# The last store of a row-wise squared deviation, split in two halves on two queues

## The chip, the cores and the metric

One core of a Trainium2 chip. The metric is the device time of one execution in microseconds, the lower the better. Kernels that are compared ran on the same chip, in alternation.

## The reference

```python
def reference(x, axis):          # x: 1024 x 4096 float32, axis = -1
    mean = np.mean(x, axis=axis, keepdims=True)
    return ((x - mean) ** 2).astype(np.float32)
```

16.78 MB are read and 16.78 MB written. There is little arithmetic for each byte.

## The kernel before

Two tiles of 128 partitions; each partition holds four rows of 4,096 numbers (65,536 B). Both tiles are loaded at the start and stay in memory. For each row VectorE sums it into a negative mean and ScalarE squares in place; of each tile's fourth row VectorE squares the last 512 columns. Each tile is stored with one DMA. Cut to what the argument touches:

```python
    for i in range(ntiles):                       # ntiles = 2
        x_tile = io.tile([P, Q * D], F32)         # Q = 4 rows, D = 4096
        if i == 0:
            nc.sync.dma_start(out=x_tile[:, :HEAD], in_=x_t[i][:, :HEAD])
            nc.sync.dma_start(out=x_tile[:, HEAD:], in_=x_t[i][:, HEAD:])
        else:
            end = Q * D - HEAD
            nc.scalar.dma_start(out=x_tile[:, end:], in_=x_t[i][:, end:])
            nc.sync.dma_start(out=x_tile[:, :end], in_=x_t[i][:, :end])
    ...
    for i in range(ntiles):
        for q in range(Q):
            row = tiles[i][:, q * D:(q + 1) * D]
            ...                                   # VectorE: neg_mean of the row
            cut = D if q < Q - 1 else LAST
            nc.scalar.activation(out=row[:, :cut], in_=row[:, :cut],
                                 func=ACT.Square, bias=neg_mean, scale=1.0)
            ...                                   # VectorE: the rest of row 3
        nc.sync.dma_start(out=out_t[i], in_=tiles[i])
```

Of the kernel before, what the change touches and what calls it, by code (L numbers as in the profile page):

```python
# [2 lines left out]

os.environ.setdefault("NEURON_RT_ULTRASERVER_MODE", "4")

# [4 lines left out]

F32 = mybir.dt.float32
ACT = mybir.ActivationFunctionType
ADD = mybir.AluOpType.add


@with_exitstack
def kernel(
    ctx: ExitStack,
    tc: tile.TileContext,
    x: bass.AP,  # L20
    axis: bass.AP,
    out: bass.AP,
):





    nc = tc.nc

    B, D = x.shape
    P = nc.NUM_PARTITIONS
    Q = 4
    HEAD = 512
    HALF = D // 2
    LAST = D - D // 8
    assert B % (P * Q) == 0
    ntiles = B // (P * Q)
    inv_d = 1.0 / float(D)

    x_t = x.rearrange("(p n q) d -> n p (q d)", p=P, q=Q)
    out_t = out.rearrange("(p n q) d -> n p (q d)", p=P, q=Q)

    io = ctx.enter_context(tc.tile_pool(name="io", bufs=ntiles))
    scratch = ctx.enter_context(tc.tile_pool(name="scratch", bufs=1))
    stats = ctx.enter_context(tc.tile_pool(name="stats", bufs=ntiles * Q))

    tiles = []
    for i in range(ntiles):
        x_tile = io.tile([P, Q * D], F32)  # L50
# [7 lines that stand above are left out]
        tiles.append(x_tile)  # L58

    inorder = tc.keep_in_program_order  # L60
# [3 lines that stand above are left out]
            pairs = scratch.tile([P, HALF], F32)  # L64
            neg_mean = stats.tile([P, 1], F32)
            inorder(nc.vector.tensor_tensor_reduce(  # L66
                out=pairs,
                in0=row[:, :HALF],
                in1=row[:, HALF:],
                scale=-inv_d,  # L70
                scalar=0.0,
                op0=ADD,
                op1=ADD,
                accum_out=neg_mean,
            ))
            cut = D if q < Q - 1 else LAST
            nc.scalar.activation(  # L77
                out=row[:, :cut],
                in_=row[:, :cut],
                func=ACT.Square,  # L80
                bias=neg_mean,
                scale=1.0,
            )
            if cut < D:
                rest = row[:, cut:]
                nc.vector.tensor_scalar_add(out=rest, in0=rest, scalar1=neg_mean)  # L86
                nc.vector.tensor_mul(out=rest, in0=rest, in1=rest)  # L87
        nc.sync.dma_start(out=out_t[i], in_=tiles[i])


# [1 line left out]
_INS = ['x', 'axis']  # L92
_OUTS = [((1024, 4096), 'float32')]

_NUMBERS = {'axis': -1}


# [26 lines left out]
```

## Time and profile before

| | before |
|---|---|
| time | 82.98 us (82.96 to 83.04, 3 runs) |
| span of the profile | 81.4 us |
| ScalarE busy, VectorE busy | 36%, 26% |
| share of 16 DMA engines' time, both queues | 96.1% |
| first store: issued, landed | 39.7, 61.2 us |
| second store: issued, landed | 58.4, 80.6 us |

"Issued" is when the issuing engine's instruction starts; "landed" is when the completion arrives. A packet is one record of a DMA engine's work in the profile; in the large stores it is one unbroken piece of a partition's data (65,536 B in the kernel before). A completion is how a DMA reports its end: 16 records of 4 B in the profile (96 of them for the six DMAs of the kernel before), and one wait in the program. The seam is the place where the packets of the first store end and those of the second begin. The time between holds all waiting behind other transfers, so a long one is no sign of a slow transfer (the second store took 22.2 us here). The lines of the page, the windows across the seam of the stores and the waits of SyncE stand in the prediction below.

### The profile page before, as it was taken

How to read it: one execution, taken by the hardware profiler on the slowest of the kernel's cores; microseconds unless marked ns; L12 is line 12 of the kernel's file. 1: busy time of each engine (PE TensorE's matmuls, PEld its weight loads, DVE VectorE, ACT ScalarE, POOL GpSimd, SP SyncE). 2: the span in 40 equal slices, each digit the busy share in tenths (PEclk: the TensorE clock that was granted, in tenths of full speed). 3: DMA queues.
4: the chain of work that ended last, by engine and by line, in shares of the span. 5: the costliest groups of instructions: out<-in, count | busy, mean ns of one | idle time of the engine just before them, and what ended most of it. 6: DMA issues, size and time to landing. Idle time of an engine off the chain costs nothing.

```text
span 81.4 us, 87 instructions
## 1 busy us (share of the span) xinstructions
DVE 20.8 (26%) x20; ACT 29.4 (36%) x9; POOL 0.2 (0%) x4
## 2 busy tenths in 40 slices
DVE  0000000000059999600039999700000000000000
ACT  0000000000054999999502999999600000000000
POOL 0000000000000000000000000000000000000000
DMA  1974999999759999995799993899996599999390
GB/s 22 704 343 187 499 499 499 499 499 437 343 218 499 499 499 499 499 406 250 343 516 515 515 515 161 354 515 515 515 516 290 258 483 515 515 515 419 161 451 0
DMA packets 864, 33.55 MB, mean 412 GB/s; under 512 B 96, under 2 KB 96, under 8 KB 352
## 3 DMA queue, kind: packets, MB, share of 16 engines
q1 hardware_dynamic: 720, 33.29, 95.0%
q10 hardware_dynamic: 144, 0.26, 1.1%
HBM read 16.78 MB, written 16.78 MB: 412 GB/s over the span
## 4 chain that ended last, share of the span: by engine, by line
DMA 49%; ACT 13%; ACTq 4%; DVE 3%; SPq 1%; issue 0%
DMA x_tile<-in_x_dram 49%; ACT x_tile L77 13%; ACTq L119 4%; DVE pairs L66 3%; SPq L53 1%; SPq L52 0%; DVE neg_mean L66 0%
## 5 line engine op out<-in xcount | busy, mean ns | idle before, releaser
L77 ACT ACTIVATE x_tile<-x_tile,neg_mean 128x4096 f32<-128x4096 f32 (+1 forms) x8 | 28.2, 3590 | 5.7 <-DVE neg_mean L66 5.7
L66 DVE CUSTOM_DVE_ANT_0 pairs<-x_tile 128x2048 f32<-128x2048 f32 x8 | 18.3, 2292 | 31.6 <-DMA x_tile<-in_x_dram 31.4
L77 ACT ACT_TABLE_LOAD x1 | 1.3, 1283 | 23.2 <-DMA x_tile<-in_x_dram 23.2
L87 DVE TENSOR_TENSOR x_tile<-x_tile 128x512 f32<-128x512 f32 x2 | 1.4, 692 | 0.1
L86 DVE TENSOR_SCALAR x_tile<-x_tile,neg_mean 128x512 f32<-128x512 f32 x2 | 1.0, 488 | 0.1
L66 DVE DVE_READ_ACCUMULATOR2_ANT neg_mean<- 128x1 f32 x8 | 0.7, 82 | 0.0
L105 POOL MEMSET const-bfloat16-1.0<- 128x1 bf16 x1 | 0.1, 102 | 0.0
L105 POOL MEMSET const-uint8-127<- 128x1 uint8 x1 | 0.1, 102 | 0.0
L105 POOL MEMSET const-float32-0.0<- 128x1 f32 x1 | 0.1, 99 | 0.2 <-issue 0.2
L105 POOL MEMSET const-float32-1.0<- 128x1 f32 x1 | 0.1, 99 | 0.0
## 6 DMA issues: line engine op xcount, KB each, us to landing
x_tile<-in_x_dram SPq DMA_DIRECT2D x2, 7936.0 KB, 31.1
x_tile<-in_x_dram ACTq DMA_DIRECT2D x1, 256.0 KB, 3.8
x_tile<-in_x_dram SPq DMA_DIRECT2D x1, 256.0 KB, 3.6
out_dram<-x_tile SPq DMA_DIRECT2D x2, 21.9
```

The costliest lines, as they stand in the source:

```text
L53: nc.sync.dma_start(out=x_tile[:, HEAD:], in_=x_t[i][:, HEAD:])
L66: inorder(nc.vector.tensor_tensor_reduce(out=pairs, in0=row[:, :HALF], in1=row[:, HALF:], scale=-inv_d, scalar=0.0, op0=ADD, op1=ADD, accu ...
L77: nc.scalar.activation(out=row[:, :cut], in_=row[:, :cut], func=ACT.Square, bias=neg_mean, scale=1.0,)
L86: nc.vector.tensor_scalar_add(out=rest, in0=rest, scalar1=neg_mean)
L87: nc.vector.tensor_mul(out=rest, in0=rest, in1=rest)
L105: nc = _bacc.Bacc("TRN2", target_bir_lowering=False, num_devices=1)
L119: with _tile.TileContext(nc) as tc:
```

## The change

The second tile's store waits for all four rows. Its first two rows are final 6.8 us earlier. The change stores them as soon as they are ready, from SyncE's queue, and the other two from ScalarE's, whose engine has nothing more to do then. The intent is an earlier start of the last store and two issuers.

```diff
-        nc.sync.dma_start(out=out_t[i], in_=tiles[i])
+        if i < ntiles - 1:
+            nc.sync.dma_start(out=out_t[i], in_=tiles[i])
+        else:
+            for queue, q in ((nc.sync, 0), (nc.scalar, 2)):
+                part = slice(q * D, (q + 2) * D)
+                queue.dma_start(out=out_t[i][:, part], in_=tiles[i][:, part])
```

## The prediction

> **What bounds the kernel now.** I read the page first: the busy shares, the slices of the DMA engines, the queues.
>
> ```profile
> DVE 20.8 (26%) x20; ACT 29.4 (36%) x9; POOL 0.2 (0%) x4
> ...
> DMA  1974999999759999995799993899996599999390
> ...
> DMA packets 864, 33.55 MB, mean 412 GB/s; under 512 B 96, under 2 KB 96, under 8 KB 352
> ...
> q1 hardware_dynamic: 720, 33.29, 95.0%
> q10 hardware_dynamic: 144, 0.26, 1.1%
> ```
>
> No compute engine is busy for more than 36% of the span. The two queues' packets fill 95.0 + 1.1 = 96.1% of the time of all 16 DMA engines. The bytes are fixed: 16.78 MB in, 16.78 MB out. So the kernel is bound by its transfers, and the question is whether any of the missing 4% lies where the second tile's store begins.
>
> The slice row seems to say so: it dips to 5 and 3 in several places, one of them at slices 29 and 30 (59 to 63 us), where the first store ends and the second begins. I did not trust this. Of the 864 packets 352 are small, so the other 512 carry nearly everything: 65,536 B each, one for each of 128 rows of four large transfers, 8 per engine per transfer. A packet takes over 2 us, longer than a slice of 2.03 us, so a packet counted in the slice where it starts makes false peaks and dips. I therefore asked for windows as long as one packet, 2.41 us, across the seam (columns: window, length, DVE, ACT, POOL, clock, DMA share, GB/s).
>
> ```profile
> 52.49:54.90 2.41, 0.00 (x0) 2.41 (x1) 0.00 (x0) 1.00 1.00 435
> 54.90:57.31 2.41, 0.00 (x0) 2.41 (x2) 0.00 (x0) 1.00 1.01 435
> 57.31:59.73 2.42, 0.00 (x0) 1.02 (x1) 0.00 (x0) 1.00 1.00 433
> 59.73:62.14 2.41, 0.00 (x0) 0.00 (x0) 0.00 (x0) 1.00 1.01 435
> 62.14:64.56 2.42, 0.00 (x0) 0.00 (x0) 0.00 (x0) 1.00 1.00 433
> ```
>
> The DMA share is 1.00 and the rate 433 to 435 GB/s in every window, before, at and after the seam. There is no hole. The instructions on the output and SyncE's waits say the same in another way:
>
> ```profile
> L88 SPq DMA_DIRECT2D out_dram<-x_tile x2: 343/346/348, 39.7 to 58.4; - x2
> ...
> DMA to landing us min/median/max: 21.5/21.9/22.2
> ```
>
> ```profile
> SPq L119 <- DMA out_dram<-x_tile: 21.7, 2, 19.3
> ```
>
> The stores were issued at 39.73 and 58.36 us (timeline). SyncE's waits at the end are 21.7 us in two parts, 2.4 and 19.3. So the first store landed some 2.4 us after the issue of the second was over (58.7 + 2.4 = 61.1 to 61.2, which is 39.7 + 21.5), and the second 19.3 us later, at 80.6 (58.4 + 22.2). One store is 128 x 65,536 B = 8.39 MB; at 434 GB/s that moves in 19.3 us. From one landing to the next there passed just the time that the bytes need. The second store took 22.2 us because for its first 2 to 3 us it stood behind the first.
>
> [...] The trace of before has a small case: in the first 3.5 us a 256 KB load from SyncE and one from ScalarE run together, and land in 3.6 and 3.8 us.
> [...] The trace doesn't show the order, but in the window 3.10 to 3.30 us, when 2,048 B packets of both queues are in flight, 410 GB/s moved, so changing queues costs at most little.
> [...]
>
> **The change, part by part.**
> - Removed: one store of 8.39 MB, issued by SyncE at 58.36 us when ScalarE ended row 3 of the second tile.
> - Added first: a store of rows 0 and 1 from SyncE. ScalarE's two activations end 7.31 us after 44.25 (chain of waits), so it can be issued at about 51.6 us, if its wait is for the part and not for the tile. I expect that, since these rows lie in columns that nothing later writes; no view of before shows it, and a rival below takes the other case. It is issued 6.8 us earlier, but the first store's packets fill all engines until about 60.9 us (landing at 61.2). It stands in the same queue behind them: gain 0.
> - Added second: a store of rows 2 and 3 from ScalarE, at 58.36 us, after its own last activation. The first load was issued at 0.73 and the first bytes flowed in the window 1.50 to 2.00, so an issue takes about 1.0 us to become traffic: the packets are there at about 59.4, before the engines are free. This was so for the old store too. Gain 0, loss 0. ScalarE has no work after it, so the 0.34 us of issue costs nothing.
> - Moved: nothing else; loads, compute and the first store stay.
> - Packet sizes: each of the 128 rows is now two packets of 32,768 B, so 8 packets more per engine. What a packet costs beyond its bytes, as an estimate: 2,048 B x 16 at 410 GB/s is 79.9 ns, at 434 GB/s 75.5 ns, so 4.4 ns. 8 x 4.4 = 0.035 us.
> - End: one more completion to wait for at the end, but both halves end together; SyncE's waits there take 17 to 28 ns each. About 0.03 us, an estimate.
> - Sum: 82.98 + 0 + 0.035 + 0.03 = 83.05 us.
>
> **The rivals.**
> - *The early half fills a hole at the seam.* The two dips in the slices speak for it, and an issue that waits for the last activation looks like a serial step. It would be worth up to the 1.0 us from issue to first bytes: 82.0 us. Against it: 433 to 435 GB/s in the window across the seam, and 19.3 us between landings for 19.3 us of bytes. Even so it would be under 2%.
> - *Two queues in turn are slower than one.* Engines would jump between two streams of writes 32 KB apart, with packets half as long. The trace has only the small packets of the first 3.5 us to judge by. In the stretch 41.9 to 61.3, where the first store begins among the last packets of a load, the mean is 432 GB/s, so mixing loads and stores cost almost nothing. If each changeover cost 50 ns, 16 of them would make 0.8 us: 83.8 us. To lose over 2% (1.66 us) the last 19.3 us would have to run 8.6% slower. Unlikely.
> - *The second issue waits longer on ScalarE's queue* (behind its last activation, on semaphores of VectorE and itself). It has about 0.9 to 1.5 us of slack before the engines are free, and even past that the early half keeps them busy: half a store is 9.7 us. This makes nothing of the time: 83.0 us.
> - *The early half waits for the whole tile after all.* Then both issues come at 58.4 us, and it is still 83.0 us.
>
> **Range and chances.** The three runs of before span 0.08 us; most of what I can think of moves the time by under 0.1 us. I take 82.85 to 83.40: the upper side is wider because only the changeover rival has size, and it can only lose. Faster by over 2% would need 81.3 us, that is, most of what lies outside the moving of bytes: 33.55 MB at 434 GB/s are 77.3 us of a span of 81.4, and the remaining 4.1 us are the start before the first bytes, the landings and the end, which the change doesn't touch. I give it 0.01. Slower by over 2%: 0.03. Within 2%: 0.96.
>
> **What would show each step.** In the changed profile: queue q1 with 29.1 MB and q10 with 4.46 MB (0.26 + 4.19), 1,008 packets in place of 864; SyncE's issue at about 51.6 us, some 28 us before it lands; ScalarE's at about 58.4 us with about 22 us to landing; both landing within about 1.3 us of each other near 80.6 (queues in turn), where a strict order of first come would land the early half at about 71; windows of 2.41 us at 433 to 435 GB/s throughout; the span at 81.4 to 81.5 us. I am wrong if the windows after 61 us show well under 430 GB/s (changeover cost), or if the last landing comes before 80.5 us (there was a hole after all).

What no trace or run of this case shows is cut from it and from one expectation below. No term of the sum is among the cuts: 82.98 + 0 + 0.035 + 0.03 = 83.05 us. That the queues would go in turn rested on one of the passages cut; the trace of the kernel before did not show the order, and the packet records of the changed kernel do ("Why the prediction was right").

## The result, and the profile after

| | before | changed |
|---|---|---|
| median | 82.98 us (82.93 to 83.04, 6 runs) | 83.15 us (83.05 to 83.33, 6 runs) |
| ratio | | 1.0022, 95% interval 1.0009 to 1.0035 |
| span of the profile | 81.4 us | 81.6 us |

Ratios here and below are the mean time of one kernel's fast runs over that of the other's of the same rounds, so not quite the ratio of the medians that stand beside them. The change costs 0.18 us (0.0022 x 82.98; interval 0.07 to 0.29), which counts as the same time at the 2% mark.

The page of the changed kernel, for packets and queues:

```profile
DMA packets 1008, 33.55 MB, mean 411 GB/s; under 512 B 112, under 2 KB 112, under 8 KB 368
...
q1 hardware_dynamic: 720, 29.10, 83.0%
q10 hardware_dynamic: 288, 4.46, 12.9%
```

The same bytes go in 144 packets more, of which 128 are data (128 rows in two pieces each) and 16 tiny ones are the added completion. ScalarE's queue q10 now has 4.46 MB. The sum of both shares is 95.9%, where it was 96.1%: the engines were full and they still are.

The instructions on the output in the changed kernel, then its list of DMA issues (issuing queue, count, KB, us from issue to landing):

```profile
L90 SPq DMA_DIRECT2D out_dram<-x_tile x1: 348/348/348, 39.6 to 39.6; - x1
L94 SPq DMA_DIRECT2D out_dram<-x_tile x1: 343/343/343, 51.5 to 51.5; - x1
L94 ACTq DMA_DIRECT2D out_dram<-x_tile x1: 347/347/347, 58.2 to 58.2; - x1
```

```profile
out_dram<-x_tile SPq DMA_DIRECT2D x1, 4096.0 KB, 28.0
out_dram<-x_tile ACTq DMA_DIRECT2D x1, 4096.0 KB, 22.4
```

The early half was issued 6.8 us before the late one, as intended. It then took 28.0 us to land, at 79.5 us; the late half took 22.4 us, to 80.7 us. The head start was spent waiting. The windows across the seam in the changed kernel show behind what (columns as in the prediction: window, length, DVE, ACT, POOL, clock, DMA share, GB/s):

```profile
54.90:57.31 2.41, 0.00 (x0) 2.41 (x2) 0.00 (x0) 1.00 1.00 435
57.31:59.73 2.42, 0.00 (x0) 0.91 (x1) 0.00 (x0) 1.00 1.00 433
59.73:62.14 2.41, 0.00 (x0) 0.00 (x0) 0.00 (x0) 1.00 1.01 435
```

The rates are the same three as before. (Of the seven windows that follow, one has 421 GB/s, the others 433 to 435. One packet of 32,768 B that falls across a window's edge is 13.6 GB/s of such a window.) The engines were at 433 to 435 GB/s with the first store's packets when the early half joined the queue, and no byte went sooner.

### The profile page after: what moved, and what is told of

The parts are those of the page before. It is cut to its first block, busy times and chain, and to the rows that moved or that the text cites. A ratio compares the mean times of both kernels' runs of the same rounds, so it can differ in the third digit from the quotient of the medians.

```text
span 81.6 us, 89 instructions
## 1 busy us (share of the span) xinstructions
DVE 20.8 (25%) x20; ACT 29.4 (36%) x9; POOL 0.2 (0%) x4
## 3 DMA queue, kind: packets, MB, share of 16 engines
q10 hardware_dynamic: 288, 4.46, 12.9%
## 4 chain that ended last, share of the span: by engine, by line
DMA 49%; ACT 14%; issue 3%; DVE 3%; SPq 1%
DMA x_tile<-in_x_dram 49%; ACT x_tile L78 14%; DVE pairs L67 3%; SPq L54 1%; SPq L53 0%; DVE neg_mean L67 0%
## 6 DMA issues: line engine op xcount, KB each, us to landing
out_dram<-x_tile ACTq DMA_DIRECT2D x1, 4096.0 KB, 22.4
```

## The experiments

My theory: the second store starts when the engines are free of the first, not when it is issued, so an earlier issue is worth nothing, and what the change adds is the cost of more packets and of one more completion. Rivals: there was a hole at the seam; turning between two queues costs; the last issue sets the end. Twelve runs were made: eleven new kernels, and the changed kernel once more. "Before" is each time the kernel before in the same rounds; its median was 83.12, 83.17 and 83.12 us on the chips of the three sets.

### Is there a hole at the seam, and is the last issue on the path?

**The second store issued 18 us early, with the first tile's data** (wrong result):

```diff
-        nc.sync.dma_start(out=out_t[i], in_=tiles[i])
+        nc.sync.dma_start(out=out_t[i], in_=tiles[0])
```

> Wrong result on purpose: the second store takes the first tile's data, which are ready at 39.7 us, so it is issued some 18 us early and stands complete in the queue before the first store ends; one store, one completion, 64 KB packets. Theory (no hole at the seam before): 82.98 within 0.06 us, ratio 0.999 to 1.001, last landing at 80.5 to 80.7 us. Rival (the late issue of the second store leaves a hole of up to 1 us in the kernel before): 82.0 to 82.7 us.

Measured: 83.11 us, ratio 0.9997 (0.9985 to 1.0009). The store was issued at 40.1 us and landed at 80.5 us, 40.4 us later:

```profile
L88 SPq DMA_DIRECT2D out_dram<-x_tile x2: 347/390/433, 39.7 to 40.1; - x2
...
DMA to landing us min/median/max: 21.5/31.0/40.4
```

Taking the wait for the data away wholly is worth nothing measurable, so the kernel before had no hole to fill. This is the strongest single evidence: the early half of the change couldn't have gained either.

**The last activation delayed by 1 us**, in the kernel before (an added activation of 1,024 columns into a scratch tile, ahead of the second tile's row 3):

```diff
+            if i == ntiles - 1 and q == Q - 1:
+                nc.scalar.activation(out=junk[:, :1024], in_=row[:, :1024],
+                                     func=ACT.Square, bias=neg_mean, scale=1.0)
             cut = D if q < Q - 1 else LAST
```

> The kernel before with an added activation of 1,024 columns ahead of the second tile's last row: the store's issue moves from 58.4 to about 59.4 us. Theory: the store has 0.9 to 1.5 us of slack before the engines are free (60.2 to 60.9), so at most 0.15 us slower: 82.98 to 83.13 us. Rival (the store's issue is on the path that sets the end): +1.0 us, 84.0 us.

Measured: 83.22 us, ratio 1.0003 (0.9985 to 1.0020). The issue moved to 59.6 us and the time did not:

```profile
L97 SPq DMA_DIRECT2D out_dram<-x_tile x2: 343/346/348, 39.8 to 59.6; - x2
```

An issue that can be late by 1.2 us is not on the path.

**The same with 4,096 columns**, in the kernel before and in the changed one:

> The kernel before with an added activation of 4,096 columns (3.6 us): issue at 62.0 us, first packets at about 63.1, while the last engine is free at 60.9. Theory: +2.0 to +2.7 us, 85.0 to 85.7 us, with a window of 2.4 us after 60.9 almost empty. Rival (some other slack hides it): under +1 us.

> The changed kernel with the same added activation of 3.6 us ahead of the last row: ScalarE's issue moves to about 61.9 us, the early half is unmoved at 51.5 us and keeps the engines busy for 9.7 us from 60.2 on. Theory: the delay is hidden wholly: 83.1 to 83.3 us, as the changed kernel without the delay. Rival (the end hangs on the last issue): 85 to 87 us.

Measured: the kernel before went to 85.47 us, ratio 1.0268 (1.0247 to 1.0288), that is 2.23 us longer; the changed kernel to 83.27 us, ratio 1.0010 (0.9993 to 1.0027) to the undelayed kernel before. The windows at the seam, first of the kernel before with the delay, then of the changed kernel with it:

```profile
57.41:59.82 2.41, 0.96 (x2) 2.38 (x2) 0.00 (x0) 1.00 1.00 435
59.82:62.23 2.41, 0.22 (x1) 2.29 (x1) 0.00 (x0) 1.00 0.00 0
62.23:64.64 2.41, 0.00 (x0) 0.00 (x0) 0.00 (x0) 1.00 1.02 435
```

```profile
57.31:59.73 2.42, 0.88 (x2) 2.39 (x2) 0.00 (x0) 1.00 1.00 433
59.73:62.14 2.41, 0.30 (x1) 2.37 (x1) 0.00 (x0) 1.00 0.95 408
62.14:64.56 2.42, 0.00 (x0) 0.00 (x0) 0.00 (x0) 1.00 1.01 433
```

This is what a real hole looks like in this view: a window in which no packet starts, 0 GB/s. In the kernel before the delayed store was issued at 62.1 us while the engines ran dry from 60.4 to 60.9 us. In the changed kernel the early half fills that place. So the split does what it was made for, but only where the last rows come late; here they come in time. The 408 is an edge effect of a few half-size packets that start on either side of the window's edge.

Finer windows of the delayed kernel before time the start of a store's traffic:

```profile
62.70:62.90 0.20, 0.00 (x0) 0.00 (x0) 0.00 (x0) 1.00 0.00 0
62.90:63.00 0.10, 0.00 (x0) 0.00 (x0) 0.00 (x0) 1.00 9.21 3932
```

Issue at 62.14, first packets between 62.9 and 63.0 (62.98 in the packet records): 0.84 us. With the last engine free at 60.9 us, the store of the kernel before, issued at 58.4, had 60.9 - 0.84 - 58.4 = 1.7 us of slack.

### What do the queues cost?

**Both halves on SyncE's queue:**

```diff
-            for queue, q in ((nc.sync, 0), (nc.scalar, 2)):
+            for queue, q in ((nc.sync, 0), (nc.sync, 2)):
```

> Both halves on SyncE's queue, rows 0-1 issued at about 51.5 us, rows 2-3 at about 58.3 us. Theory (the engines have no hole at the seam; the +0.17 us of the change is 8 more packets per engine at some 5 ns and one more completion to wait for at the end): as the changed kernel within 0.1 us, so 83.05 to 83.2 us, ratio to the kernel before 1.0005 to 1.003; the halves come one after the other, the first lands near 71 us, the second near 80.6. Rival (turning between two queues is what costs): back to 82.98 us within 0.04, ratio below 1.0008.

Measured: 83.38 us, ratio 1.0033 (1.0010 to 1.0057), 0.27 us over before with an interval of 0.08 to 0.47. The halves landed at 71.0 and 80.7 us, one after the other. The rival (two queues are the cost) would have brought this back to before; it did not. But the six runs spread from 83.05 to 83.80 us, more than any other kernel here, and the median missed the expected 83.2 us. By the times it says only that two queues are not needed for the cost. The traces say more: the packets of the second store take the engines 19.42 us here, and 19.39 and 19.41 us in the two profiles of the changed kernel (table below), so turning between two queues shows no cost of its own in the changed kernel.

**The early half on ScalarE's queue, right after row 1; the late half on SyncE's:**

```diff
+            if i == ntiles - 1 and q == 1:
+                nc.scalar.dma_start(out=out_t[i][:, :2 * D], in_=tiles[i][:, :2 * D])
 ...
+            nc.sync.dma_start(out=out_t[i][:, 2 * D:], in_=tiles[i][:, 2 * D:])
```

> The early half goes out on ScalarE's queue right after row 1, the late half on SyncE's: the early half then does not stand behind the first store but shares the engines with it in turn from about 52.5 us. Theory (only the sum of bytes counts): the first store lands later, at about 68 to 70 us in place of 61.2, the last at 80.6 to 80.9, and the time is as the changed kernel within 0.15 us, 83.0 to 83.3 us; ScalarE may lose up to 0.5 us at the issue. Rival (mixing queues slows the engines): over 83.5 us.

Measured: 83.20 us, ratio 1.0003 (0.9986 to 1.0021). On a queue of its own the early half did not stand behind the first store; it went in turn with it. Its first packets began 4.2 to 6.6 us after its issue, for each engine first ended the packet it was at and one or two more of the first store. Landing times of the three stores in that kernel:

```profile
DMA to landing us min/median/max: 22.2/25.2/26.4
```

The first store (issued at 39.6) landed at 64.8 us, some 3.5 us later than before, the early half (51.5) at 77.9, the late one (58.3) at 80.5. The time is the same, so the order in which the bytes went didn't matter here, only their sum. My 68 to 70 us for the first store was wrong: I shared the engines out by bytes, and from 52.5 us on. They went in turn by packet. On the three engines that came last the first store still had two 64 KB packets and its completion to send, and in the packet records each of the three stands behind one 32 KB packet of the other queue: 3 x 1.2 = 3.6 us.

### What do packets and completions cost?

**Eight stores of half a row**, four on each queue:

```diff
-            for queue, q in ((nc.sync, 0), (nc.scalar, 2)):
-                part = slice(q * D, (q + 2) * D)
+            for n in range(8):
+                queue = nc.sync if n < 4 else nc.scalar
+                part = slice(n * D // 2, (n + 1) * D // 2)
```

> Eight stores of half a row each, four on SyncE's queue, four on ScalarE's: 16,384 B packets, 32 for each engine where the kernel before has 8, and seven more completions. Theory: 24 x 5 ns = 0.12 us for packets, plus 0 to 0.4 us for the waits at the end (0.06 each if all stand behind the last landing): 83.1 to 83.5 us. Rival (each change of queue costs tens of ns): 32 changes at 50 ns, 1.6 us: above 84 us.

**One store in eight pieces of half a row**, reversed so that the pieces stay apart (64 packets per engine, where the kernel before has 8):

```diff
-            nc.sync.dma_start(out=out_t[i], in_=tiles[i])
+            o = out_t[i].rearrange("p (h d) -> p h d", h=8)
+            s = tiles[i].rearrange("p (h d) -> p h d", h=8)
+            nc.sync.dma_start(out=o[:, ::-1], in_=s[:, ::-1])
 ... (for the second tile; the first tile's store stays)
```

> The second store as one DMA whose rows go out in eight pieces of 8,192 B each, in reversed order, so that they can't be merged: 64 packets per engine in place of 8, the packet size of the eight stores before it, but one completion and one queue. (The 16,384 B and 32 packets named in the expectation of the eight stores were a slip: half a row is 8,192 B.) Theory: 56 packets x 5 to 6 ns = 0.28 to 0.34 us, and no extra wait at the end: +0.25 to +0.4 us, 83.3 to 83.5 us, ratio 1.003 to 1.005. Rival (the queues and completions are the cost of the eight stores, not the packets): within 0.1 us of before. If it is +0.8 us as with the eight stores, packets are the whole of it.

Measured: the eight stores 83.92 us, ratio 1.0097 (1.0083 to 1.0111), 0.81 us over before; the one reversed store 83.73 us, ratio 1.0072 (1.0056 to 1.0088), 0.60 us over before. Both were above what I expected (83.1 to 83.5, and 83.3 to 83.5). In the same 16.90 us after the seam, first of the kernel before, then of the one reversed store, then of the eight stores:

```profile
62.14:79.04 16.90, 0.00 (x0) 0.00 (x0) 0.00 (x0) 1.00 1.00 434
```

```profile
62.14:79.04 16.90, 0.00 (x0) 0.00 (x0) 0.00 (x0) 1.00 1.01 424
```

```profile
62.14:79.04 16.90, 0.00 (x0) 0.00 (x0) 0.00 (x0) 1.00 1.01 421
```

One queue gives 424 GB/s and two queues in turn 421, against 434 with 64 KB packets. So the packets are most of the cost. The changed kernel has 432 GB/s in this window and 434 in its repeat: one of its packets at the edge is 1.9 GB/s, too coarse for so small a cost.

The packet records give a finer measure, with no window's edge in it: the time from the end of the first store's last data packet to the last completion record, as a mean over the 16 engines. Each is one profile; the rows with 8 packets agree within 0.01 us, those with 16 within 0.03.

| kernel | packets per engine | us |
|---|---|---|
| before | 8 | 19.34 |
| halves by even and odd partitions (below) | 8 | 19.33 |
| changed, and its repeat | 16 | 19.39, 19.41 |
| both halves on SyncE's queue | 16 | 19.42 |
| one reversed store | 64 | 19.83 |
| eight stores | 64 | 19.94 |

What one more packet costs comes out as 8 to 11 ns, an estimate in each case. By the times: 0.60 us for 56 more packets per engine is 10.7 ns each (8.3 to 13.1 over the interval). By this table: 0.49 us, 8.8 ns each. By the rates: 8,192 B x 16 x (1/424 - 1/434) = 7.1 ns for each of 64 pieces, so 0.46 us, 8.1 ns for each of the 56 added. Turning between queues at every packet is, by these two profiles, at most the 0.1 us between the last two rows, under 2 ns a packet.

The rest of what the eight stores cost above the one is at the end. SyncE's drain, an instruction of the program's end, comes after its waits for all completions; its first start, in the kernel before, the changed one, the one reversed store and the eight stores:

```profile
L119 SPq DRAIN  x3: 7/7/7, 80.7 to 81.0; - x3
```

```profile
L125 SPq DRAIN  x3: 7/7/7, 80.8 to 81.1; - x3
```

```profile
L124 SPq DRAIN  x3: 7/7/7, 81.2 to 81.5; - x3
```

```profile
L126 SPq DRAIN  x3: 7/7/7, 81.6 to 81.9; - x3
```

To the nanosecond, in the records of SyncE: from its last wait that a landing released to the drain it takes 68 ns in the kernel before and 67 in the reversed store, 127 in the changed kernel and 253 with eight stores, because one and three more waits stand in the program behind that wait, though what they wait for is already there. So 59 ns more in the changed kernel and 186 more with eight stores. A further 0.02 us comes after the drain in every kernel with more completions: from SyncE's first drain at the end to the end of the span it is 0.71 us in the kernel before and the reversed store, 0.73 in the changed kernel and with eight stores, and GpSimd's instruction that clears the semaphores takes 92 and 93 ns there in place of 74. For the eight stores the table gives 0.60 us over before, and 0.60 + 0.19 + 0.02 = 0.81 us is what was measured. The agreement is closer than the noise of 0.1 us warrants. (With eight stores SyncE's last issue also waited 9.7 us for the first store's completion and started at 61.7 us; the engines had packets all the while.)

**The halves by partition**, each with 64 KB packets:

```diff
-            nc.sync.dma_start(out=out_t[i], in_=tiles[i])
+            for lo in (0, P // 2):
+                ps = slice(lo, lo + P // 2)
+                nc.sync.dma_start(out=out_t[i][ps], in_=tiles[i][ps])
 ... (for the second tile; the first tile's store stays)
```

> The second store as two of 64 partitions each, both on SyncE's queue after the last activation: packets stay 65,536 B, so no packet cost (880 packets in place of 864, the 16 more are of 4 B), but one more issue and one more completion. Theory: the part of the 0.17 us that is the extra completion, 0.03 to 0.08 us; 83.0 to 83.07 us. Rival (half-size packets are the whole cost): 82.98 within 0.03. Rival 2 (the early issue of a half matters): as before or slower by the second issue, 0.4 us.

Measured: 103.78 us, ratio 1.2484 (1.2468 to 1.2500). I had looked for 0.05 us and found 20.7. Each half takes its own 19.8 us (windows of this kernel: the seam, the first half, the second):

```profile
57.31:59.73 2.42, 0.00 (x0) 1.02 (x1) 0.00 (x0) 1.00 1.07 433
60.20:80.00 19.80, 0.00 (x0) 0.00 (x0) 0.00 (x0) 1.00 1.02 215
80.00:99.90 19.90, 0.00 (x0) 0.00 (x0) 0.00 (x0) 1.00 0.96 207
```

The engines are busy all the time (share 1.02, 0.96) and move half the bytes: a packet takes 5.11 us (median) in place of 2.42. Two things are new in these stores: each has 64 partitions, and they are neighbours. That makes a test: 64 partitions again, but the even and the odd ones.

**The halves by even and odd partitions:**

```diff
-            for lo in (0, P // 2):
-                ps = slice(lo, lo + P // 2)
-                nc.sync.dma_start(out=out_t[i][ps], in_=tiles[i][ps])
+            for lo in (0, 1):
+                nc.sync.dma_start(out=out_t[i][lo:P:2], in_=tiles[i][lo:P:2])
```

> The second store as two of 64 partitions each again, but the even and the odd partitions in place of the lower and the upper half; both on SyncE's queue after the last activation. Theory[...] the packets go back to 2.42 us, and the time is 83.0 to 83.3 us. Rival (two DMAs of 64 partitions are slow whatever the partitions, for instance because of 4 packets per engine or of the second issue's 1.3 us): about 104 us again.

Measured: 83.20 us, ratio 1.0008 (0.9987 to 1.0029). Full rate again, with the same number of DMAs, partitions, packets and the same issuer:

```profile
62.14:79.04 16.90, 0.00 (x0) 0.00 (x0) 0.00 (x0) 1.00 1.00 434
```

So what made the difference (103.78 against 83.20 us) is which partitions a DMA holds, not how many. By what mechanism is not shown. The rows in DRAM change with the partitions, and no run changed one without the other. This kernel also does what the first was meant for: two completions, 64 KB packets, the first completion long there when the last comes, and a cost that can't be told from zero (0.07 us, -0.11 to 0.24).

### The changed kernel again, and the start of the kernel

> The changed kernel once more, on another chip and beside the three below, to have a firmer size of its cost. Theory: 0.05 to 0.25 us over the kernel before of the same rounds (ratio 1.0006 to 1.003). If the 0.17 us of the first measurement was chance, the ratio lies within 0.9995 to 1.0005.

Measured: 83.28 us, ratio 1.0019 (1.0004 to 1.0034): 0.16 us. The small cost shows again in a second set of rounds (chip 8), with an interval clear of zero.

**One load per tile** in the kernel before (four loads become two):

```diff
-            nc.sync.dma_start(out=x_tile[:, :HEAD], in_=x_t[i][:, :HEAD])
-            nc.sync.dma_start(out=x_tile[:, HEAD:], in_=x_t[i][:, HEAD:])
+            nc.sync.dma_start(out=x_tile, in_=x_t[i])
 ... (the second tile likewise)
```

> The kernel before with one load per tile, in place of the two with small first pieces: aimed not at the change but at what is left outside the moving of bytes. The first 3.5 us move 2,048 B packets at well under 434 GB/s. Theory (bytes and the ends are all there is): up to 0.5 us faster, 82.5 to 83.0 us. Rival (the small pieces start the engines earlier than a large load would): 83.0 to 83.5 us.

Measured: 83.19 us, ratio 1.0006 (0.9993 to 1.0020). No gain, so the expected 0.5 us was not there to be had: the small first pieces aren't why the first microseconds are slow. In the packet records of this kernel the first 64 KB packets begin at 1.74 us and take up to 3.46 us each, where later ones take 2.42, so the start is slow with large packets too. Why is open. No experiment gave a version that beats the kernel before.

## Why the prediction was right

- **Bound by the DMA engines, no hole at the seam.** Right. The early issue with other data (ratio 0.9997) takes the wait away altogether and gains nothing. In detail I slipped in three places. Only the packets of the two stores have 65,536 B; those of the two large loads have 63,488. In the stretch 41.9 to 61.3 us there was no mixing of loads and stores to judge by: the last packet of a load ended at 41.5 us. And counted from 0, the dip that I put at slices 29 and 30 (59 to 63 us) stands at slices 30 and 31 (61 to 65 us), just behind the seam. It is the false dip either way, for the windows show 433 to 435 GB/s there.
- **The early half gains nothing.** Right: issued at 51.5 us (predicted 51.6), so its wait was for the part and not for the tile; landed at 79.5.
- **The late half loses nothing.** Right, and the slack was larger than I said: 1.7 us to the last engine in place of 0.9 to 1.5, because the issue became traffic in 0.84 us (timed in the delayed kernel), not the 1.0 that I had read off the start of the kernel. The two delays bracket it: 1.2 us later costs nothing, 3.7 us later costs 2.23 us.
- **Queues in turn.** Right: on 15 of the 16 engines the packet records alternate between the two queues from the third packet on, on one from the fourth, until the early half has no more; the halves land 1.2 us apart (predicted within 1.3), and the packets of two queues in turn take the engines no longer than those of two halves on one queue (19.39 and 19.41 against 19.42 us). The rival with 50 ns for each change is out.
- **The sum.** The right terms, both too small. Packets: predicted 8 x 4.4 ns = 0.035 us; the two profiles of the changed kernel have 0.04 and 0.07 in the table of packet records, and the reversed store's time gives 8 x 10.7 = 0.086. The 4.4 ns came from 2,048 B packets in a window of 0.2 us, too short for a difference of a few ns. Completion: predicted 0.03 us from the length of one wait; in the trace 0.059 before the drain and 0.02 after it. So 0.12 to 0.17 us in place of 0.065, against measured 0.18 (0.07 to 0.29) and 0.16 (0.03 to 0.28). The measured time, 83.15 us, lies in the range and 0.10 us above the point.
- **The signs.** All came but two that were off by a little: the span is 81.6 us in place of 81.4 to 81.5 (the profiled run was the slowest of the six), and one window after the seam has 421 GB/s. That the time stayed within 2% is weak evidence by itself, for every rival on the list stayed within 2% too; it is the experiments that set the theory apart from them.
- **Not settled.** Whether another few hundredths come from elsewhere, the noise of 0.1 us doesn't allow to say. Both halves on one queue cost 0.27 us (0.08 to 0.47) without the late extra wait, where packets and the 0.02 us after the drain would give 0.06 to 0.11; that fits only at the edge of its interval.

## What to carry to other kernels

Before you hurry an issue, ask what its transfer stands behind: where landings followed each other by just the time of the bytes (19.3 us for 8.39 MB here), an issue 18 us earlier bought slack and no time (ratio 0.9997). Look at the DMA rate in windows as long as one packet, since windows shorter than a packet show holes that are not there: in the kernel before, windows of 0.5 us have 1,835 GB/s at 58.0 to 58.5 us and 0 from 58.5 to 60.0, where those of 2.41 us have 433 to 435. Splitting a store cost a little here for every packet (8 to 11 ns at 8,192 B, an estimate) and every completion that the end waits for behind the last landing (59 ns for one, 186 for three), and splitting it into halves of 64 neighbouring partitions cost 20.7 us, by even and odd partitions 0.07 us (-0.11 to 0.24).
